# The S5 table stage of a two-block kernel: its transfers issued from GpSimd's queue instead of SP's

## The chip, the cores and the metric

One Trainium2 chip; the kernel uses one core of it. The metric is the device time of the kernel in microseconds. Times of a profile are counted from the start of the profiled execution's span.

## What is computed

Two blocks, one after the other, on a sequence of 512 tokens of width 1024, in fp32. The first is a conformer-like block; the second has retention, an S5 branch and cross-attention:

```python
# first block
x = layer_norm(a*x + 0.5*(1 + g1)*swiglu(modulate(x, sh1, sc1), ffn1...), ...)
...                                     # recurrent and convolution branches, mixed
x = layer_norm(a*x + 0.5*(1 + g3)*swiglu(modulate(x, sh3, sc3), ffn2...), ...)
# second block
ret = retention(q, k, v, ret_gn_g) * silu(g_ret)
ssm = s5_branch(u, a_re, a_im, log_dt, b_re, b_im, c_re, c_im, d, glu_w, glu_b) * silu(g_s5)
x = x + concatenate([ret, ssm]) @ w_out
...                                     # cross-attention on 256 memory tokens
return rms_norm(x, norm_f_g)
```

The S5 branch is a diagonal complex recurrence, of 64 groups with 64 states each:

```python
dt = exp(log_dt)
abar = exp(a*dt)                        # complex: a = a_re + i*a_im
f = (abar - 1) / a
bb = f * b                              # per group, state and input
x[t] = abar * x[t-1] + bb @ u[t]
y = re(c @ x)
```

## The kernel before

**Weights.** Nearly all the time is matmuls of 128x512 tiles in three passes: a weight tile of 128x1024 is loaded raw (512 KB, four buffers, `wr`), ScalarE rounds it to its high part (`wh`, L147), VectorE forms the rest (`wl`, L133), and TensorE multiplies high by high, high by low and low by high: 24 matmuls for one chunk of 128 output columns. `prep` (L165) does this, two chunks ahead of TensorE. Every transfer of the kernel goes through `load` (L129), which issues it from SP, the sync engine. SP takes its list in order: a transfer that waits (a load for a free buffer, a store for the value) holds up all that stand behind it.

**Feed-forward.** `ffn` (L424) runs in three parts of 8, 8 and 6 column blocks. Of each part first the gate and up chunks (two for each block), then eight down chunks. After each chunk `pump` (L251) takes steps of other work from a background list.

**The S5 tables.** The second block's S5 branch needs tables made from a, dt, b and c alone. `s5_tables` (L1041) returns them as steps, put into that list by `after_first` (L977), so they are made under the second feed-forward (877 to 1236 us):

- `small`: loads a_re, a_im and log_dt (two halves) and works out powers of abar and f in some 92 operations, most of 128x32, on VectorE, with two sines on ScalarE. The scheduler puts it much earlier in the program than where it is written.
- `rows`: turns products of the powers with f by TensorE and stores them to DRAM as Fd (four stores).
- `bb`: loads b, makes the input table, stores it as BBd (four), and loads c.
- eight chunks of b: `b_load` loads two tiles from Fd, each row spread over 16 partitions (256 KB), and two tiles of bt as halves (128 KB each); `b_chunk` makes two tiles by six products and sums of 128x512 on GpSimd; `store` stores them to Bd.
- eight chunks of c: `c_chunk` makes two tiles from memsets (L1190) and twelve 64x256 operations on GpSimd; `store` stores them to Cd.

Cd and BBd come back in `s5_kernels` (L1221), for the S5 kernels: its first six reloads of Cd and four of BBd are issued from SP ahead of the last part's down chunks (`before_last`, L1003), and the scheduler moves them into SP's list between weights. The tiles `s` are slots of one pool that all steps share, so a reload waits until the earlier holder of its slot is stored. The order on each engine is the scheduler's, by the program's data flow, not the order of the code.

Of the kernel before, what the change touches and what calls it, by code (L numbers as in the profile page):

```python
# [16 lines left out]
S = 512  # L17
# [1023 lines left out]
def s5_tables(n):  # L1041


    nc, a = n.nc, n.a
    g = nc.gpsimd
    st = {}
    n.Fd = n.DT([2, 8, 32 * 128], "Fd")
    n.Bd = n.DT([8, 2, 128, S], "Bd")
    n.Cd = n.DT([8, 2, 128, S], "Cd")
    n.BBd = n.DT([4, 128, S], "BBd")  # L1050

    def small():
        ar, ai, dt, t, mag, sn, cs, fr, fi = (n.C([128, 32], name="s5") for _ in range(9))
        n.load(ar, a["s5_a_re_2"])
        n.load(ai, a["s5_a_im_2"])
        for p in range(2):
            n.load(dt[p * 64:(p + 1) * 64, :], a["s5_log_dt_2"][p].partition_broadcast(64))
        dt = accurate_exp(n, dt, 32)
        n.tt(mag, ar, dt, ALU.mult)
        mag = accurate_exp(n, mag, 32)  # L1060
        n.tt(fr, ai, dt, ALU.mult)
        reduced(n, fr, t, 32)
        sincos(n, sn, cs, fr)
        P = [n.C([128, 5, 32], name="pw") for _ in range(2)]
        nc.vector.memset(P[0][:, 0, :], 1.0)
        nc.vector.memset(P[1][:, 0, :], 0.0)
        n.tt(P[0][:, 1, :], mag, cs, ALU.mult)
        n.tt(P[1][:, 1, :], mag, sn, ALU.mult)
        t2 = n.C([128, 2, 32], name="pw2")
        for w in (1, 2):  # L1070
            b = [P[j][:, w, :].unsqueeze(1).to_broadcast([128, w, 32]) for j in range(2)]
            cmul(n, P[0][:, 1 + w:1 + 2 * w, :], P[1][:, 1 + w:1 + 2 * w, :], P[0][:, 1:1 + w, :], P[1][:, 1:1 + w, :],
                 b[0], b[1], t2[:, 0:w, :])
        n.s5P = P

        n.q4r, n.q4i = n.C([128, 8, 32], name="q4"), n.C([128, 8, 2, 32], name="q4i")
        Q = n.q4r, n.q4i[:, :, 1, :]
        for j in range(2):
            nc.vector.tensor_copy(out=Q[j][:, 0, :], in_=P[j][:, 4, :])
        s3 = n.A()  # L1080
        t3 = s3[:, 0:128].rearrange("p (k q) -> p k q", k=4)
        for w in (1, 2, 4):
            b = [Q[j][:, w - 1, :].unsqueeze(1).to_broadcast([128, w, 32]) for j in range(2)]
            cmul(n, Q[0][:, w:2 * w, :], Q[1][:, w:2 * w, :], Q[0][:, 0:w, :], Q[1][:, 0:w, :], b[0], b[1], t3[:, 0:w, :])
        n.F(s3)
        n.ts(n.q4i[:, :, 0, :], Q[1], -1.0)
        nP = n.C([128, 4, 32], name="npw")
        n.ts(nP, P[1][:, 0:4, :], -1.0)

        nr = n.C([128, 32], name="nr")  # L1090
        n.ts(nr, P[0][:, 1, :], -1.0, op0=ALU.add)
        ni = P[1][:, 1, :]
        den = mag
        n.tt(den, ar, ar, ALU.mult)
        n.tt(t, ai, ai, ALU.mult)
        n.tt(den, den, t, ALU.add)
        nc.vector.reciprocal(out=den, in_=den)
        n.tt(fr, nr, ar, ALU.mult)
        n.tt(t, ni, ai, ALU.mult)
        n.tt(fr, fr, t, ALU.add)  # L1100
        n.tt(fr, fr, den, ALU.mult)
        n.tt(fi, ni, ar, ALU.mult)
        n.tt(t, nr, ai, ALU.mult)
        n.tt(fi, fi, t, ALU.subtract)
        n.tt(fi, fi, den, ALU.mult)
        st.update(f=(fr, fi), nP=nP)

    def rows():

        P = n.s5P  # L1110
        fr, fi = (x.unsqueeze(1).to_broadcast([128, 4, 32]) for x in st["f"])
        G = [n.A() for _ in range(3)]
        p, h, t = (x[:, 0:128].rearrange("p (k q) -> p k q", q=32) for x in G)
        cmul(n, p, h, P[0][:, 1:5, :], P[1][:, 1:5, :], fr, fi, t)
        for r, x in enumerate((p, h)):
            ps = n.ST()
            for j in range(4):
                n.mm(ps[0:32, j * 128:(j + 1) * 128], x[:, 3 - j, :], n.ident)
            o = n.A()
            n.act(o[0:32, :], ps[0:32, :], AF.Copy)  # L1120
            for p in range(2):
                n.load(n.Fd[r, p * 4:p * 4 + 4].rearrange("k (q x) -> q k x", q=32),
                       o[0:32, :].rearrange("q (k x) -> q k x", k=4))
            n.F(o)
        n.F(G)

    def b_load(ch):

        E, B = ([n.A() for _ in range(2)] for _ in range(2))
        cols = slice(ch * S, (ch + 1) * S)  # L1130
        for r in range(2):
            n.load(E[r], n.Fd[r][:, cols].unsqueeze(1).to_broadcast([8, 16, S]))
            for p in range(2):
                n.load(B[r][p * 64:(p + 1) * 64],
                       a[("s5_bt_re", "s5_bt_im")[r]][ch, p].unsqueeze(0).to_broadcast([4, 16, S]))
        st["b", ch] = E, B

    def b_chunk(ch):
        E, B = st.pop(("b", ch))
        O, T = n.A(), n.A()  # L1140
        n.tt(O, E[0], B[0], ALU.mult, g)
        n.tt(T, E[1], B[1], ALU.mult, g)
        n.tt(O, O, T, ALU.subtract, g)
        n.tt(T, E[0], B[1], ALU.mult, g)
        n.tt(B[0], E[1], B[0], ALU.mult, g)
        n.tt(T, T, B[0], ALU.add, g)
        n.F(E, B)
        st["out", ch] = n.Bd, (O, T)

    def store(ch):  # L1150
        d, X = st.pop(("out", ch))
        for r in range(2):
            n.load(d[ch % 8, r], X[r])
        n.F(X)

    def bb():

        b = [n.A() for _ in range(2)]
        for r in range(2):
            n.load(b[r], a[("s5_bn_re", "s5_bn_im")[r]])  # L1160
        fr, fi = (x.unsqueeze(2).to_broadcast([128, 32, 16]) for x in st["f"])
        br, bi = (x.rearrange("p (c q) -> p c q", q=16) for x in b)
        o = [n.A() for _ in range(3)]
        orr, oi, t = (x.rearrange("p (c q) -> p c q", q=16) for x in o)
        cmul(n, orr, oi, br, bi, fr, fi, t, g)
        for r, x in enumerate((orr, oi)):
            for h in range(2):
                d = n.A()
                g.memset(d, 0.0)
                dv = d.rearrange("p (c r q) -> p c r q", r=2, q=16)  # L1170
                for p in range(2):
                    nc.vector.tensor_copy(out=dv[p * 64:(p + 1) * 64, :, p, :],
                                          in_=x[p * 64:(p + 1) * 64, h * 16:(h + 1) * 16, :])
                n.load(n.BBd[r * 2 + h], d)
                n.F(d)
        n.F(b, o)
        c = [n.A() for _ in range(2)]
        for r in range(2):
            n.load(c[r], a[("s5_c_re", "s5_c_im")[r]])
        n.ts(c[1], c[1], -1.0)  # L1180
        st["c"] = c

    def c_chunk(ch):

        P, nP = n.s5P, st["nP"]
        q = slice(ch * 4, ch * 4 + 4)
        sh = [64, 4, 4, 16]
        X = [n.A() for _ in range(3)]
        for r in range(2):
            g.memset(X[r], 0.0)  # L1190
        for par in range(2):
            d = slice(par * 64, (par + 1) * 64)
            bc = lambda x: x[d].rearrange("p k q -> p q k").unsqueeze(3).to_broadcast(sh)
            pr, pi, npi = bc(P[0][:, 0:4, q]), bc(P[1][:, 0:4, q]), bc(nP[:, :, q])
            cr, nci = (x[d, ch * 64:(ch + 1) * 64].rearrange("p (c x) -> p c x", x=16).unsqueeze(2).to_broadcast(sh)
                       for x in st["c"])
            orr, oi, t = (x.rearrange("p (c r k x) -> p c r k x", c=4, r=2, k=4)[d, :, par] for x in X)
            n.tt(orr, pr, cr, ALU.mult, g)
            n.tt(t, pi, nci, ALU.mult, g)
            n.tt(orr, orr, t, ALU.add, g)  # L1200
            n.tt(oi, pr, nci, ALU.mult, g)
            n.tt(t, npi, cr, ALU.mult, g)
            n.tt(oi, oi, t, ALU.add, g)
        n.F(X[2])
        st["out", 8 + ch] = n.Cd, X[0:2]
        if ch == 7:
            n.F(st.pop("c"))

    work = [(9, lambda ch=ch: b_chunk(ch)) for ch in range(8)] + [(10, lambda ch=ch: c_chunk(ch)) for ch in range(8)]
    steps = [(10, small), (8, rows), (8, bb), (0, lambda: b_load(0))]  # L1210
    for i in range(17):
        if i < 7:
            steps.append((0, lambda i=i: b_load(i + 1)))
        if i < 16:
            steps.append(work[i])
        if i:
            steps.append((0, lambda i=i: store(i - 1)))
    return steps
# [709 lines left out]
```

## Time and profile before

| | |
|---|---|
| three runs | 1840.8, 1843.66, 1845.17 us (median 1843.66) |
| profiled execution, own time | 1847.32 us |
| its span | 1845.5 us |
| granted TensorE clock, mean over the span | 0.988 |
| busy: TensorE, VectorE, ScalarE, GpSimd | 97%, 66%, 37%, 17% of the span |
| HBM read and written | 239 MB and 21 MB, 141 GB/s over the span |
| transfers issued, by engine | all by SP |

The span is the profiled execution from its first to its last instruction; its own time is 1.8 us longer. A share of busy time is an average over stages; for the change the stretch of the second feed-forward, and the start, are read by themselves.

### The profile page before, as it was taken

Reading aid. Unit: us, or ns where it says so; the run is one execution under the profiler, and the core shown is the slowest. Engines: PE = TensorE matmul, PEld = TensorE weight load, DVE = VectorE, ACT = ScalarE, POOL = GpSimd, SP = SyncE. Lnnn points to the kernel's source line nnn. Section 1 sums busy time; section 2 is a strip of 40 time slices with the busy share of each in tenths; the row PEclk is TensorE's granted clock in tenths of the full one; section 3 lists DMA queues with packets and bytes.
Section 4 is the critical chain, followed back from the end, with each engine's and each line's share of the span. In section 5 each row is a group of like instructions: output and inputs, shape, how many; then the busy total and the mean of one; then the engine's idle time right before and its main releaser. Section 6 shows DMA issues by size and latency. Waiting matters only on the chain.

```text
span 1845.5 us, 21756 instructions
## 1 busy us (share of the span) xinstructions
PE 1784.5 (97%) x8242; PEld 1469.6 (80%) x8242; DVE 1219.0 (66%) x1915; ACT 682.9 (37%) x931; POOL 322.7 (17%) x292
## 2 busy tenths in 40 slices
PE   5999999999999999898999999999999999999997
PEld 4888888888877888688887788888888777888886
DVE  7888634378999999768343434357389677356644
ACT  4422323233378522434321222235351223644442
POOL 2000001030000000234145880415000010012102
PEclk9999999999999999899999999999999999999999
DMA  8888432334222223244664444454633225744211
GB/s 319 304 316 319 146 115 97 89 109 146 93 91 69 92 98 113 77 146 136 189 191 132 148 154 152 143 176 102 194 114 102 70 74 171 222 144 131 80 47 57
DMA packets 105352, 261.45 MB, mean 142 GB/s; under 512 B 15008, under 2 KB 32032, under 8 KB 105120
## 3 DMA queue, kind: packets, MB, share of 16 engines
q1 hardware_dynamic: 105248, 260.07, 42.9%
q8 instruction: 64, 1.05, 0.2%
q14 instruction: 40, 0.33, 0.1%
HBM read 239.19 MB, written 20.84 MB: 141 GB/s over the span
## 4 chain that ended last, share of the span: by engine, by line
PE 78%; POOL 7%; DMA 6%; DVE 4%; ACT 2%; issue 2%; SPq 1%; DVEq 0%; POOLq 0%; ACTq 0%
PE ps L152 75%; POOL s L133 6%; PE st L152 3%; DMA s<-in_s_bt_im 2%; DVE s L133 1%; ACT s L147 1%; SPq L130 1%; DMA s<-in_s_bt_re 1%; DVE ar L391 1%; DVE s L136 1%; DMA wr<-in_ffn_w_down 1%; DMA s<-Fd 1%; DMA wr<-in_ffn_w_gate 1%; DVE wl L133 0%; POOL s L143 0%
## 5 line engine op out<-in xcount | busy, mean ns | idle before, releaser
L152 PE MATMUL ps<-s,wh 128*128 128x512 f32 (+1 forms) x4272 | 1324.3, 392 | 11.7 <-ACT wh L147 6.6
L152 PEld LDWEIGHTS ps<-s,wh 128*128 128x128 f32 x4272 | 802.3, 189 | 183.7 <-ACT wh L147 9.9
L152 PE MATMUL ps<-s,wl 128*128 128x512 f32 (+1 forms) x2136 | 832.5, 390 | 3.3 <-DVE wl L133 3.3
L147 ACT ACTIVATE wh<-wr 128x1024 fp32r<-128x1024 f32 (+1 forms) x277 | 289.6, 1047 | 845.5 <-PE ps L152 506.4
L133 DVE TENSOR_TENSOR wl<-wr,wh 128x1024 fp32r<-128x1024 f32 (+1 forms) x277 | 354.2, 1279 | 210.9 <-ACT wh L147 205.6
L152 PEld LDWEIGHTS ps<-s,wl 128*128 128x128 f32 x2136 | 403.4, 189 | 88.8 <-DVE wl L133 5.5
L133 POOL TENSOR_TENSOR s<-s,s 128x512 f32<-128x512 f32 (+2 forms) x152 | 202.5, 1337 | 632.1 <-DVE s L136 326.0
L133 DVE TENSOR_TENSOR s<-s,s 128x512 fp32r<-128x512 f32 (+2 forms) x265 | 205.5, 783 | 55.4 <-ACT s L147 54.3
L147 ACT ACTIVATE s<-s 128x512 fp32r<-128x512 f32 (+3 forms) x246 | 153.2, 637 | 192.5 <-DVE s L133 99.6
L152 PE MATMUL ps<-s,s 128*128 128x512 f32 (+7 forms) x648 | 149.8, 381 | 20.7 <-ACT s L147 18.6
L136 DVE SCALAR_TENSOR_TENSOR s<-s,s,s 128x503 f32<-128x503 f32 (+26 forms) x240 | 164.1, 745 | 0.7
L152 PEld LDWEIGHTS ps<-s,s 128*128 128x128 f32 (+2 forms) x648 | 106.8, 177 | 58.1 <-ACT s L147 21.2
L133 DVE TENSOR_TENSOR s<-s,ps 128x512 f32<-128x512 f32 (+1 forms) x61 | 40.7, 669 | 134.9 <-PE ps L152 134.9
L136 DVE SCALAR_TENSOR_TENSOR s<-ps,c,s 128x512 f32<-128x512 f32 x56 | 41.9, 748 | 82.9 <-PE ps L152 82.7
L391 DVE SCALAR_TENSOR_TENSOR ar<-ar,silc 128x1024 f32<-128x1024 f32 x72 | 89.4, 1252 | 9.7 <-DMA ar<-in_ada_w 9.1
L147 ACT ACTIVATE s<-ps 128x512 f32<-128x512 f32 (+2 forms) x147 | 85.3, 588 | 15.5 <-PE ps L152 15.0
L133 DVE TENSOR_TENSOR s<-ps,s 128x512 f32<-128x512 f32 (+4 forms) x80 | 46.8, 616 | 61.8 <-PE ps L152 41.8
L284 POOL TENSOR_TENSOR gs<-gs,mhalf 128x4 f32<-128x4 f32 x8 | 11.0, 1371 | 259.6 <-DVE gs L141 259.6
L152 PE MATMUL st<-s,s 128*128 128x127 f32 (+2 forms) x368 | 51.5, 297 | 4.4 <-ACT s L147 3.1
L152 PEld LDWEIGHTS st<-s,s 128*128 128x128 f32 x368 | 47.9, 197 | 8.1 <-ACT s L147 3.6
L133 DVE TENSOR_TENSOR s<-s,st 128x512 f32<-128x512 f32 x73 | 46.6, 681 | 11.5 <-PE st L273 11.1
L284 POOL TENSOR_TENSOR ls<-ls,mhalf 128x4 f32<-128x4 f32 x4 | 4.5, 1133 | 259.9 <-DVE ls L136 259.9
(157 smaller groups left out, 884.7 us busy)
## 6 DMA issues: line engine op xcount, KB each, us to landing
wr<-in_w_in SPq DMA_DIRECT2D x80, 512.0 KB
ar<-in_ada_w SPq DMA_DIRECT2D x72, 512.0 KB
wr<-in_ffn_w_gate SPq DMA_DIRECT2D x44, 512.0 KB
wr<-in_ffn_w_up SPq DMA_DIRECT2D x44, 512.0 KB
wr<-in_ffn_w_down SPq DMA_DIRECT2D x32, 512.0 KB
s<-Cd SPq DMA_DIRECT2D x32, 256.0 KB
wr<-in_w_out SPq DMA_DIRECT2D x16, 512.0 KB
wr<-in_ffn_w_down SPq DMA_DIRECT2D x16, 384.0 KB
```

Of the source, the lines that this page charges most:

```text
L130: self.nc.sync.dma_start(out=out, in_=in_)
L133: (eng or self.nc.vector).tensor_tensor(out=out, in0=a, in1=b, op=op)
L136: self.nc.vector.scalar_tensor_tensor(out=out, in0=a, scalar=s, in1=b, op0=op0, op1=op1)
L147: self.nc.scalar.activation(out=out, in_=in_, func=f, scale=scale)
L152: self.nc.tensor.matmul(out, lhsT=lhsT, rhs=rhs, start=start, stop=stop)
L284: self.nc.gpsimd.tensor_tensor(out=out, in0=v, in1=self.mhalf[:, 0:n], op=ALU.pow)
L391: n.nc.vector.scalar_tensor_tensor(out=w, in0=w, scalar=1.0, in1=n.silc, op0=ALU.mult, op1=ALU.mult, accum_out=n.mod[:, j:j + 1])
```

## The change

A helper in `s5_tables` issues a transfer from GpSimd, and every transfer of the stage goes through it: 96 of the 682 that SP had. The reloads of Cd and BBd, and all weights, stay on SP. One line is added, so lines behind L1046 count one higher.

```diff
     g = nc.gpsimd
+    move = lambda out, in_: g.dma_start(out=out, in_=in_)
...
-        n.load(ar, a["s5_a_re_2"])
-        n.load(ai, a["s5_a_im_2"])
+        move(ar, a["s5_a_re_2"])
+        move(ai, a["s5_a_im_2"])
         for p in range(2):
-            n.load(dt[p * 64:(p + 1) * 64, :], a["s5_log_dt_2"][p].partition_broadcast(64))
+            move(dt[p * 64:(p + 1) * 64, :], a["s5_log_dt_2"][p].partition_broadcast(64))
...
         for r in range(2):
-            n.load(E[r], n.Fd[r][:, cols].unsqueeze(1).to_broadcast([8, 16, S]))
+            move(E[r], n.Fd[r][:, cols].unsqueeze(1).to_broadcast([8, 16, S]))
             for p in range(2):
-                n.load(B[r][p * 64:(p + 1) * 64],
+                move(B[r][p * 64:(p + 1) * 64],
                        a[("s5_bt_re", "s5_bt_im")[r]][ch, p].unsqueeze(0).to_broadcast([4, 16, S]))
...
         for r in range(2):
-            n.load(d[ch % 8, r], X[r])
+            move(d[ch % 8, r], X[r])
```

The same replacement is made at the stores of Fd and BBd and at the loads of b and c.

The scheduler then gives other orders. VectorE's list at its start, where `tiny`, `pw`, `m` and `rg` are small constants and vectors and s_6505 is the tile of log_dt:

```order
 L743 MEMSET tiny_2785 128x1
-L1065 MEMSET pw_6586 128x32
-L1066 MEMSET pw_6587 128x32
+L1066 MEMSET pw_6586 128x32
+L1067 MEMSET pw_6587 128x32
+L143 TENSOR_SCALAR s_6505<-s_6505 128x32
 L141 TENSOR_SCALAR m_104<-vecs_84 128x8
 L141 TENSOR_SCALAR rg_2789<-vecs_84 128x8
```

The first operation of `small`, which needs log_dt, now stands ahead of all work on the vectors `vecs`; the others of `small` follow between the sums for the modulation (L391), and ScalarE's two sines move there too. Before, they stood in the first feed-forward.

GpSimd's list in the chunks of b, from the store of one chunk to the first products of another:

```order
+L1046 DMA Bd<-s_7251 128x512
+L1046 DMA Bd<-s_7252 128x512
+L1046 DMA s_7479<-in_s_bt_re 64x1x512 x2
+L1046 DMA s_7478<-Fd 128x1x512
+L1046 DMA s_7595<-in_s_bt_re 64x1x512 x2
+L1046 DMA s_7594<-Fd 128x1x512
+L1046 DMA s_7242<-Fd 128x1x512
 L133 TENSOR_TENSOR s_7372<-s_7242,s_7244 128x512
+L1046 DMA s_7243<-in_s_bt_re 64x1x512 x2
 L133 TENSOR_TENSOR s_7371<-s_7241,s_7243 128x512
 L133 TENSOR_TENSOR s_7371<-s_7371,s_7372 128x512
```

Transfers now stand between the products, some of them loads of later chunks and some, as s_7242 and s_7243, of the product right behind. In this list a transfer also waits for the one eight before it on the same queue, whose semaphore it uses again.

SP's list near the end of the gate and up chunks of the second part, where wr_8074 is the fifteenth of sixteen:

```order
 L130 DMA wr_8005<-in_ffn_w_gate 128x1024
-L130 DMA Cd<-s_8110 128x512
-L130 DMA Cd<-s_8495 128x512
-L130 DMA Cd<-s_8496 128x512
 L130 DMA wr_8038<-in_ffn_w_up 128x1024
 L130 DMA s_9047<-Cd 128x512
 L130 DMA s_9050<-Cd 128x512
 L130 DMA wr_8074<-in_ffn_w_gate 128x1024
-L130 DMA Cd<-s_8233 128x512
-L130 DMA Cd<-s_8234 128x512
-L130 DMA Cd<-s_8616 128x512
+L130 DMA wr_8126<-in_ffn_w_up 128x1024
```

The stores are gone from here; the two reloads of Cd stay where they were, and wait for GpSimd's stores of s_8495 and s_8496, whose slots they take. On GpSimd 55 transfers (12 of Fd, 20 of bt, 16 of Bd, 7 of Cd) stand between the first product of the b chunks and the end of the store of s_8496.

## Rows read from the trace of the kernel before

**Rows 1.** The page, part 1: busy time of each engine, share of the span, instructions

```profile
PE 1784.5 (97%) x8242; PEld 1469.6 (80%) x8242; DVE 1219.0 (66%) x1915; ACT 682.9 (37%) x931; POOL 322.7 (17%) x292
```

**Rows 2.** Five stretches: busy time and instructions of each engine, clock, DMA share, GB/s

```profile
core 0: us, PE busy (x) PEld busy (x) DVE busy (x) ACT busy (x) POOL busy (x), PEclk, DMA share, GB/s
0.00:42.45 42.45, 21.97 (x73) 15.70 (x73) 30.84 (x95) 18.06 (x30) 12.12 (x13) 1.00 0.86 318
913.10:1038.30 125.20, 116.76 (x491) 94.08 (x490) 47.35 (x42) 29.10 (x34) 72.02 (x53) 0.96 0.58 167
1038.30:1101.80 63.50, 63.50 (x282) 52.59 (x281) 24.95 (x22) 15.73 (x20) 58.07 (x74) 1.00 0.36 125
913.10:1087.00 173.90, 165.46 (x706) 134.40 (x705) 67.09 (x59) 41.70 (x50) 116.65 (x107) 0.97 0.51 152
1100.00:1150.00 50.00, 49.01 (x216) 39.95 (x215) 20.09 (x20) 12.59 (x14) 10.16 (x13) 1.00 0.48 170
```

**Rows 3.** The chain of waits, 880 to 1130 us: start us, us, what

```profile
912.51 14.18 DMA s<-in_s_bt_im
...
961.24 12.49 DMA s<-in_s_bt_re
...
991.60 9.84 DMA s<-Fd
...
1010.23 9.79 DMA wr<-in_ffn_w_gate
...
1068.57 2.10 DMA Cd<-s
...
1102.03 3.78 DMA wr<-in_ffn_w_up
```

**Rows 4.** Waits of SP's queue: waited for: us in total, times, longest us

```profile
SPq L130 <- DVE wl L133: 1001.0, 212, 23.5
SPq L130 <- POOL s L133: 142.1, 33, 15.4
```

**Rows 5.** VectorE's timeline, start and near 200 us: start, us, what, [idle before]

```profile
5.86 0.17 DVE L141 TENSOR_SCALAR m<-vecs 128x8 f32<-128x8 f32 x1 [4.78 <-DMA vecs<-in_vecs]
...
197.22 0.18 DVE L143 TENSOR_SCALAR s<-s 128x32 f32<-128x32 f32 x1
197.44 0.18 DVE L143 TENSOR_SCALAR ex<-s 128x32 f32<-128x32 f32 x1
...
207.45 0.19 DVE L133 TENSOR_TENSOR pw<-pw,pw 128x32 f32<-128x32 f32 x1
207.55 0.19 DVE L133 TENSOR_TENSOR ex<-s 128x32 f32<-128x32 f32 x1
...
211.67 0.19 DVE L133 TENSOR_TENSOR s<-s,ex 128x32 f32<-128x32 f32 x1
```

**Rows 6.** SP's timeline, 1015 to 1130 us

```profile
1087.91 1.66 SPq L130 DMA_DIRECT2D s<-Cd  x2
...
1102.03 0.39 SPq L130 DMA_DIRECT2D wr<-in_ffn_w_up  x1
```

**Rows 7.** GpSimd's timeline, 900 to 1180 us

```profile
913.12 1.30 POOL L133 TENSOR_TENSOR s<-s,s 128x512 f32<-128x512 f32 x1 [38.03 <-PE ps L152]
...
1152.65 2.23 POOL L133 TENSOR_TENSOR s<-pw,s 64x256 f32<-64x256 f32 x2 [41.62 <-PE ps L152]
```

**Rows 8.** Issues by tile, Fd and Cd: duration ns min/median/max, first and last start

```profile
L130 SPq DMA_DIRECT2D s<-Fd x16: 577/614/852, 906.4 to 1009.0; - x16
...
L130 SPq DMA_DIRECT2D Cd<-s x16: 319/326/327, 1055.4 to 1174.0; - x16
```

**Rows 9.** The page, part 5: GpSimd's costliest group, busy us, mean ns, idle before

```profile
L133 POOL TENSOR_TENSOR s<-s,s 128x512 f32<-128x512 f32 (+2 forms) x152 | 202.5, 1337 | 632.1 <-DVE s L136 326.0
```

**Rows 10.** TensorE's timeline, at the start and near 1108 us

```profile
22.45 8.57 PE L152 MATMUL ps<-s,s 128*128 128x512 f32 x24 [3.56 <-ACT s L147]
32.43 5.74 PE L152 MATMUL ps<-s,s 128*128 128x512 f32 x24 [1.41 <-ACT s L147]
...
1108.75 0.50 PE L152 MATMUL ps<-s,wl 128*128 128x512 f32 x1 [0.99 <-DVE wl L133]
```

More of the change, by code (lines that the diff above doesn't have):

```diff
@@ L1121, in rows @@
             for p in range(2):
-                n.load(n.Fd[r, p * 4:p * 4 + 4].rearrange("k (q x) -> q k x", q=32),
+                move(n.Fd[r, p * 4:p * 4 + 4].rearrange("k (q x) -> q k x", q=32),
                        o[0:32, :].rearrange("q (k x) -> q k x", k=4))
@@ L1159, in bb @@
         for r in range(2):
-            n.load(b[r], a[("s5_bn_re", "s5_bn_im")[r]])
+            move(b[r], a[("s5_bn_re", "s5_bn_im")[r]])
         fr, fi = (x.unsqueeze(2).to_broadcast([128, 32, 16]) for x in st["f"])
@@ L1173, in bb @@
                                           in_=x[p * 64:(p + 1) * 64, h * 16:(h + 1) * 16, :])
-                n.load(n.BBd[r * 2 + h], d)
+                move(n.BBd[r * 2 + h], d)
                 n.F(d)
@@ L1178, in bb @@
         for r in range(2):
-            n.load(c[r], a[("s5_c_re", "s5_c_im")[r]])
+            move(c[r], a[("s5_c_re", "s5_c_im")[r]])
         n.ts(c[1], c[1], -1.0)
```

## The prediction

> **What bounds the kernel now.** I read the page first: TensorE is busy for 1784.5 of the 1845.5 us span and GpSimd for 322.7 [rows 1]. So a change that touches no matmul can win only where TensorE waits, and can lose wherever it makes TensorE wait. Then I cut the second feed-forward into stretches. From the first product of the Bd tables (913.1 us) to 1038.3 us, TensorE ran 491 matmuls in 125.2 us; in the 63.5 us behind that, 282 at full clock without a pause, 0.2252 us each [rows 2]. At that pitch 491 take 110.6 us: **14.6 us are lost**, partly as idle time, partly at the lower clock that is granted after it (a mean of 0.96 in that stretch). Another 1.0 us is idle between 1100 and 1150 us [rows 2]. The recoverable sum is 15.6 us.
>
> Who lost it? The chain of waits through the same time goes through GpSimd's products and through transfers that take long to land: 14.18 us and 12.49 us for loads of bt, 9.84 us for a load of Fd, and 9.79 us for a weight that stood behind them [rows 3]. The queue's own waits say why weights come late: SP waits mostly for a weight buffer, its usual life (1001.0 us), but for another 142.1 us it waits for GpSimd to finish a product that SP is to store [rows 4], and every weight behind that store waits too.
>
> **What the change takes away.** 96 of SP's transfers go; SP then holds weights and reloads. SP stands no longer in front of a store until the product is there. I take the whole 15.6 us as gone: its places are those where a weight stood behind a table's transfer. The lower end of this gain is nothing, since the same bytes still cross the same DMA engines beside the weights.
>
> **What it adds at the start.** Four loads are GpSimd's first work, and the scheduler moves the short arithmetic on a and dt from 197.22 to 211.86 us, where VectorE had gaps, to the front of VectorE's list, ahead of all that works on the vectors [rows 5]. VectorE had begun there at 5.86 us [rows 5]. Four issues at 1 us from about 0.8 us on, and a landing like the 3.78 us of a weight [rows 3], put dt at 8.6 us: 2.7 us later. The roughly 92 short operations behind it cost 0.1 to 0.2 us each (see their starts in [rows 5]), 9 to 18 us, against 11.6 us that VectorE stood idle in the first 42.45 us [rows 2]. I add 0.8 us for that: **+3.5 us**. The ends are 0 (dt lands before the vectors) and 10 (2.7, and 18 less 11.6 not hidden). At 197 us nothing is won, since TensorE did not wait for it.
>
> **What it adds in the second feed-forward.** This term decides. GpSimd now issues 55 transfers (12 of Fd, 20 of bt, 16 of Bd, 7 of Cd) between its first product and the last Cd store for which SP waits. In SP's order two reloads of Cd, s_9047 and s_9050, come right ahead of wr_8074, the fifteenth of sixteen gate and up chunks of the second part. They go into buffers that GpSimd's tables held and wait for its stores. Before, GpSimd had 57.3 us idle among 173.9 us up to there (116.65 busy) [rows 2], and SP got to the reloads at 1087.91 us [rows 6], with TensorE never stopping for long. Now the list is one after the other on GpSimd:
>
> - the products and memsets, unchanged: 913.1 + 116.65 [rows 2, 7];
> - 55 issues at c each. No row shows a transfer issued by GpSimd. SP took 0.61 us for one of Fd and 0.33 for one of Cd [rows 8]; a GpSimd operation on a whole tile takes 1.34 us [rows 9]. I take **c = 1.0 us**, about the middle of 0.61 and 1.34; the ends are 0.35 and 1.34;
> - landings that nothing covers. Four places: s_7242, s_7243 and s_7477 are loaded right ahead of their products, and the run of issues ahead of s_7242 waits for transfers eight before. At 3.78 us each [rows 3]: 15.1 us. At the low end they are hidden under the issues; at the high end all 57.3 us of idle time stay;
> - the landing of the last store, 2.10 us [rows 3], and 0.4 us for the reload's issue.
>
> That is 913.1 + 116.65 + 55 + 15.1 + 2.5 = 1102.3 us for the issue of wr_8074. From such an issue to steady matmuls it took 6.7 us (1102.03 to 1108.75) [rows 6, 10]: 1109.0 us. TensorE wants it much earlier. Before, it was through with that chunk at about 1107.2 and so began it near 1101.8; with 14.6 us recovered it is there at 1087.2. **The new stall is 21.8 us.** After it the clock is low for a while: after such a pause at the start, 24 matmuls took 8.57 us and the next 24 took 5.74 [rows 10], so +2.8 us.
>
> The Trainium skill, "DMA: Bandwidth & Descriptors", section "Latency and other measured facts", gives about 0.6 us to the first byte from the hardware path and about 1 us from GpSimd's, where it calls the excess the cores' emission. If that 1 us is GpSimd's own time, the sum is the one above; if it is only a delay of the transfer, GpSimd is held for less and the third case below follows. No run here shows it.
>
> Behind that point GpSimd has 9 more Cd stores, about 9 us, and ahead of its last products it stood idle for 41.62 us waiting for TensorE [rows 7]: that covers them, and if it were gone they would hold up the next reloads of Cd in the third part.
>
> **Sum.** 21.8 + 2.8 + 3.5 - 15.6 = +12.5 us. The profiled execution's own time was 1847.32 us, 3.7 above the median of 1843.66; with the sum it would be 1859.8, and against the median **1856 us**. As a formula the change is 55c - 42.5 us: zero at c = 0.77, and 5.5 us for each 0.1 us of c. About 0.2% (3.7 us) is what the measurement can tell from no change.
>
> **Rivals.**
>
> 1. Landings stay as slow as before, and GpSimd waits for them and issues as well. For it: the bt loads are halves of a tile that took 12 to 14 us to land [rows 3], and nothing in the change makes them smaller. Against: they queued behind weights in one queue. All 57.3 us in place of 15.1: +42.2, so 1898 us.
> 2. The other side: an issue costs GpSimd no more than SP. At c = 0.61 the list ends 21.5 us earlier, the new stall is 0.3 us and needs no warming; with +3 at the start, 0.3 + 3 - 15.6 = -12.3, so 1831 us. For it: the same descriptor work, and GpSimd idle a third of the time. Against: every GpSimd operation that shows its cost is slower than its counterpart elsewhere. It decides from c = 0.77 down.
> 3. The change does not do what it says for TensorE: weights land late because the DMA engines are busy, not because of SP's order; GpSimd issues in its idle third, and nothing moves but the start: +3.5 us at most, 1844 to 1847 us. For it: 167 GB/s in the bad stretch against 125 behind it [rows 2]. Against: 318 GB/s at the start [rows 2].
>
> The Trainium skill's page "DMA: Bandwidth & Descriptors", section "Issuing engines are not separate DMA queues", says that an issue from another engine only saves sequencer time, because all run on the same 16 DMA engines. By that rule alone the third case would hold; the 142.1 us of SP standing before stores [rows 4] is sequencer time that the rule itself allows to be saved.
>
> **How the numbers follow.** The forecast, with c between 0.85 and 1.34 (1848 to 1875 us), 0.5; rival 1, 0.2; rival 2, 0.2; rival 3, 0.1. Range: 1829 us, just below rival 2, to 1900, just above rival 1; outside lie c under 0.4 together with hidden landings, and slow landings together with c over 1. The likeliest case's own range is 1848 to 1875. Faster by over 0.2%: 0.2 (rival 2). Within: 0.1. Slower: 0.7 (the forecast and rival 1).
>
> **What would show it.** Right: GpSimd's gaps from 913 us on are about as long as the issues that stand in them; SP waits for GpSimd at the two reloads of Cd for some 15 to 25 us; TensorE shows one long gap near 1087 us, ended by the weight split of wr_8074, and almost none from 913 to 1038. The four issues at 0.8 us come before VectorE's first work on vectors, and steady matmuls begin 2 to 5 us later than 42.45. Wrong: the gap near 1087 is missing (c is small), or TensorE waits for weights between 913 and 1038 as before (rival 3), or GpSimd's idle time ends on loads of Fd and bt rather than on issues (rival 1).

## The result and the profile after

The changed kernel takes **1857.64 us** (median of 4 runs, 1854.63 to 1861.8); the kernel before took 1842.3 us beside it. The ratio is 1.0084, with a 95% interval of 1.0066 to 1.0102: slower by 15 us. The forecast was 1856. The profiled execution is the longest of the four (1861.8 us); it spans 1860.0 us, 14.5 more than that of before.

The page's part 1 and part 3 show what moved: GpSimd is busy for 49 us more, because a transfer that it issues counts as its work, and a second DMA queue exists.

```profile
PE 1782.5 (96%) x8242; PEld 1470.7 (79%) x8242; DVE 1234.6 (66%) x1915; ACT 682.6 (37%) x931; POOL 372.1 (20%) x388
...
q1 hardware_dynamic: 94112, 240.88, 39.2%
q0 software_dynamic: 10368, 19.22, 3.8%
```

**The gain came.** The same stretches as in [rows 2], and one more, of the changed kernel:

```profile
0.00:42.45 42.45, 15.64 (x43) 10.44 (x44) 33.46 (x167) 16.90 (x29) 12.66 (x17) 0.97 0.79 284
...
913.10:1038.30 125.20, 125.20 (x554) 103.66 (x553) 55.66 (x47) 32.24 (x39) 88.51 (x91) 1.00 0.68 180
1038.30:1101.80 63.50, 53.21 (x234) 43.42 (x232) 28.77 (x16) 11.07 (x14) 57.42 (x76) 0.97 0.22 73
...
916.80:1103.10 186.30, 174.71 (x770) 144.03 (x768) 83.65 (x61) 43.31 (x52) 143.90 (x162) 0.99 0.51 142
```

From 913 to 1038 us TensorE does 554 matmuls without a pause, at full clock, where it did 491. In the next stretch it stands still for 10.3 us, where it stood for none. The last row is GpSimd's own list, from its first product to the Cd store that SP waits for: 162 instructions, the 107 of before and the 55 transfers.

**The stall came too.** Waits of SP's queue, against [rows 4]:

```profile
SPq L130 <- DVE wl L133: 1159.3, 241, 23.5
...
SPq L130 <- DMA Cd<-s: 58.6, 4, 46.0
...
SPq L130 <- POOL s L133: 27.6, 7, 10.6
```

The 142.1 us of standing before products are 27.6 now; in their place SP stands once for 46.0 us before a Cd store has landed. The timelines of SP and TensorE show where, against [rows 6, 10]:

```profile
1057.94 0.33 SPq L130 DMA_DIRECT2D wr<-in_ffn_w_up  x1
1104.45 1.17 SPq L130 DMA_DIRECT2D s<-Cd  x2
1105.72 0.37 SPq L130 DMA_DIRECT2D wr<-in_ffn_w_gate  x1
...
1117.30 0.33 SPq L130 DMA_DIRECT2D s<-BBd  x1
...
1093.26 0.39 PE L152 MATMUL ps<-s,wl 128*128 128x512 f32 x1
1111.77 1.22 PE L152 MATMUL ps<-s,wh 128*128 128x512 f32 x2 [18.12 <-ACT wh L147]
```

After the fourteenth weight of the part SP issues nothing from 1058 to 1104 us, because the two reloads of Cd stand first in its list. wr_8074 goes out at 1105.72, and TensorE, which was ready for it at 1093.65, stands for 18.12 us.

**The start came later**, against [rows 5, 10]; timelines of GpSimd, VectorE and TensorE:

```profile
2.58 1.07 POOL L1046 DMA_DIRECT2D s<-in_s_log_dt  x2
...
9.19 0.18 DVE L143 TENSOR_SCALAR s<-s 128x32 f32<-128x32 f32 x1 [8.09 <-DMA s<-in_s_log_dt]
9.28 0.16 DVE L141 TENSOR_SCALAR m<-vecs 128x8 f32<-128x8 f32 x1
...
38.14 7.37 PE L152 MATMUL ps<-s,s 128*128 128x512 f32 x24 [3.28 <-ACT s L147]
```

Behind its first memsets VectorE goes on at 9.19 instead of 5.86 us, with the operation that needs log_dt. A run of 24 matmuls that began at 32.43 begins at 38.14.

The n-th matmul of one trace can be paired with the n-th of the other, each counted from the start of its span. The difference can then be followed through the kernel:

| at, us of the changed kernel | later than before, us | what happened |
|---|---|---|
| 50 to 700 | 7.2 | the start |
| 870 | 7.9 | |
| 890 to 970 | 3.9 | 4.0 won: the kernel before had waited 0.8 and 1.1 us near 876 us, with a granted clock of 0.50 for 3.4 us behind that |
| 1030 | -10.4 | 14.3 won |
| 1060 | -7.9 | 2.4 lost, most of it in a wait of 2.1 us for a weight's split |
| 1111.77 | 10.3 | 18.3 lost in the long gap |
| 1118 | 13.5 | 3.2 lost at a lower clock, some 13 matmuls |
| 1130 | 12.2 | 1.3 won: the kernel before had a short wait of its own |
| the end | 14.3 | |

The row of the slow matmuls behind the gap, with a granted clock of 0.50:

```profile
1111.77:1118.00 6.23, 6.19 (x14) 4.41 (x15) 3.98 (x4) 1.89 (x3) 5.58 (x8) 0.50 0.23 84
```

### The profile page after: what moved, and what is told of

The parts are those of the page before. It is cut to its first block, busy times and chain, and to the rows that moved or that the text cites. A ratio compares the mean times of both kernels' runs of the same rounds, so it can differ in the third digit from the quotient of the medians.

```text
span 1860.0 us, 21759 instructions
## 1 busy us (share of the span) xinstructions
PE 1782.5 (96%) x8242; PEld 1470.7 (79%) x8242; DVE 1234.6 (66%) x1915; ACT 682.6 (37%) x931; POOL 372.1 (20%) x388
## 4 chain that ended last, share of the span: by engine, by line
PE 80%; POOL 8%; DMA 4%; DVE 3%; issue 2%; ACT 1%; SPq 1%; DVEq 0%; POOLq 0%; ACTq 0%
PE ps L152 76%; POOL s L133 6%; PE st L152 3%; DMA s<-Fd 1%; POOL s L1046 1%; DVE s L133 1%; SPq L130 1%; ACT s L147 1%; DVE s L136 1%; DMA Bd<-s 1%; DVE ar L391 0%; POOL Bd L1046 0%; PE st L273 0%; DMA s<-Cd 0%; DMA s<-in_s_log_dt 0%
## 5 line engine op out<-in xcount | busy, mean ns | idle before, releaser
L152 PE MATMUL ps<-s,wh 128*128 128x512 f32 (+1 forms) x4272 | 1321.0, 391 | 21.8 <-ACT wh L147 18.1
L133 DVE TENSOR_TENSOR wl<-wr,wh 128x1024 fp32r<-128x1024 f32 (+1 forms) x277 | 367.3, 1327 | 195.1 <-ACT wh L147 189.3
L133 DVE TENSOR_TENSOR s<-s,s 128x512 fp32r<-128x512 f32 (+1 forms) x265 | 205.1, 782 | 50.0 <-ACT s L147 48.8
L152 PE MATMUL ps<-s,s 128*128 128x512 f32 (+7 forms) x648 | 150.6, 382 | 27.1 <-ACT s L147 23.8
L391 DVE SCALAR_TENSOR_TENSOR ar<-ar,silc 128x1024 f32<-128x1024 f32 x72 | 87.1, 1221 | 8.2 <-DMA ar<-in_ada_w 7.7
L147 ACT ACTIVATE s<-ps 128x512 f32<-128x512 f32 (+2 forms) x147 | 85.2, 587 | 15.5 <-PE ps L152 14.9
```

What stands on the lines that cost most here:

```text
L133: (eng or self.nc.vector).tensor_tensor(out=out, in0=a, in1=b, op=op)
L147: self.nc.scalar.activation(out=out, in_=in_, func=f, scale=scale)
L152: self.nc.tensor.matmul(out, lhsT=lhsT, rhs=rhs, start=start, stop=stop)
L391: n.nc.vector.scalar_tensor_tensor(out=w, in0=w, scalar=1.0, in1=n.silc, op0=ALU.mult, op1=ALU.mult, accum_out=n.mod[:, j:j + 1])
```

## The experiments

Nine kernels, all against the kernel before on the same chip, which took 1841.84 to 1842.35 us each time, so that times of different runs can be set beside each other. Times are medians; the changed kernel took 1857.64 us. Where an expectation says 6.7 us for the later start, the pairing above gives 7.2.

### The start by itself

```diff
-        move(ar, a["s5_a_re_2"])
-        move(ai, a["s5_a_im_2"])
+        n.load(ar, a["s5_a_re_2"])
+        n.load(ai, a["s5_a_im_2"])
         for p in range(2):
-            move(dt[p * 64:(p + 1) * 64, :], ...)
+            n.load(dt[p * 64:(p + 1) * 64, :], ...)
```

> The four loads of `small` go back to SP, the other 92 transfers stay on GpSimd. In the changed kernel TensorE's matmuls run 6.7 us later than before from 47 us on, and I put all of this down to VectorE's list beginning with an operation on log_dt that waits for GpSimd's transfer (until 9.19 us, where the vectors had been there at 5.86). Theory (the start is lost for good, and what follows keeps its distances): steady matmuls begin as before, everything behind them comes 6 to 7 us earlier, 1851 us. Rival (the later stall takes up what the start gives: GpSimd's list begins at a fixed time, TensorE only waits longer near 1090 us): the gap there grows from 18 to about 25 us, and the time stays within 2 us of 1857.6.

Measured: 1851.79 us, ratio 1.0051 (1.0033 to 1.0068). TensorE's start and its waits under the second feed-forward:

```profile
0.00:42.45 42.45, 21.96 (x74) 15.74 (x75) 31.17 (x95) 18.41 (x30) 12.10 (x13) 1.00 0.86 320
```

```profile
PE ps L152 <- ACT wh L147: 17.7, 1, 17.7
```

The start is that of before (21.97 us busy in [rows 2], 21.96 here), and the gap is as long as in the changed kernel: GpSimd's list came earlier with everything else, its first product at 911.28 us instead of 916.83. The start is a loss by itself, of 5.9 us in the median. The rival falls.

### Which reloads stop SP

```diff
     def load():
         st["bb"] = [n.A() for _ in range(4)]
         for i, d in enumerate(st["bb"]):
             n.load(d, n.BBd[i])
         for ch in range(3):
-            fetch(ch)
+            fetch(ch, n.nc.gpsimd)
-    def fetch(ch):
+    def fetch(ch, eng=n.nc.sync):
         st[ch] = [n.A(), n.A()]
         for r in range(2):
-            n.load(st[ch][r], n.Cd[ch, r])
+            eng.dma_start(out=st[ch][r], in_=n.Cd[ch, r])
```

> The first six reloads of Cd are issued from GpSimd as well, so that none of them stands on SP ahead of wr_8074; the reloads of BBd stay on SP, the first of them ahead of the first down chunk, two chunks later. Theory (whatever SP must wait for behind GpSimd's list stops TensorE): the gap ahead of the fifteenth chunk goes, and a gap of 15 to 22 us comes two chunks later, ahead of the first down chunk, because the first reload of BBd waits for a store that GpSimd issued at 1117.6 us; time 1855 to 1860 us, no gain. Rival (only the two reloads of Cd were the trouble): no gap over 5 us, 1833 to 1838 us.

Measured: 1863.99 us, ratio 1.0103 (1.0078 to 1.0128); its profiled execution took 1855.07. TensorE's waits, and SP's timeline:

```profile
PE ps L152 <- ACT wh L147: 17.5, 1, 17.5
```

```profile
1068.20 0.33 SPq L130 DMA_DIRECT2D wr<-in_ffn_w_up  x1
1115.23 0.33 SPq L130 DMA_DIRECT2D s<-BBd  x1
1115.65 1.36 SPq L130 DMA_DIRECT2D wr<-in_ffn_w_down  x3
```

SP gets two weights further (1068.20) and then stands for 47 us before the first reload of BBd. The gap moved by two chunks and is as long. In the end it waits for a product of GpSimd and not, as expected, for the store behind that product: the reload goes out at 1115.23, the store at 1115.50. No gain, as the theory had it, but the median lies above its 1855 to 1860 us. The other executions took about 1863 to 1865 us, some 9 us more than the one with the profile; the trace of that one cannot show why, and it stays open.

Now the reloads of BBd as well:

```diff
         for i, d in enumerate(st["bb"]):
-            n.load(d, n.BBd[i])
+            n.nc.gpsimd.dma_start(out=d, in_=n.BBd[i])
```

> All ten early reloads, six of Cd and four of BBd, are issued from GpSimd; SP then has only weights there. Theory: the two small gaps and the long one near 1090 us (2.2 + 18.4 us) and the slow matmuls behind it (3.2 us) go: 1857.6 - 23.8 = about 1834 us, which is under the 1842.3 of the kernel before. Rival (weights come late because GpSimd's transfers use the same DMA engines, and SP's wait is only where it shows): TensorE waits for weights elsewhere, 1850 us or more.

Measured: **1835.02 us**, ratio 0.9964 (0.9948 to 0.9981). The stretches:

```profile
913.00:1038.00 125.00, 125.00 (x553) 103.48 (x553) 61.76 (x46) 32.09 (x39) 86.61 (x93) 1.00 0.71 180
1038.00:1130.00 92.00, 92.00 (x408) 76.17 (x407) 46.02 (x35) 24.44 (x31) 83.77 (x111) 1.00 0.47 148
```

TensorE does not stop at all in these 217 us. 22.6 us are back, of the 23.8 that the theory counted, with ten more transfers on GpSimd. So neither GpSimd's load nor the sharing of the DMA engines slows TensorE here: ten reloads in SP's list did.

### Does issuing set the pace of GpSimd's list?

```diff
             move(d[ch % 8, r], X[r])
+            if d is n.Bd:
+                move(n.Bx[ch % 8, r], X[r])
```

> Each of the 16 stores of Bd is issued a second time, to another place in DRAM that nothing reads: 16 more issues on GpSimd at 0.60 us, 9.6 us, all ahead of the Cd stores for which SP waits. Theory (GpSimd's list is one after the other, issues and products and waits, and its end sets when wr_8074 may go): the end comes 9 to 11 us later, time 1866 to 1869 us. Rival (landings set the pace and issues lie in their shadow): under 3 us later, 1857 to 1861 us. If more than 13 us are added, the transfers' landings and the rule that each waits for the one eight before cost more than the issues themselves.

Measured: 1862.05 us, ratio 1.0106 (1.0089 to 1.0123): 4.4 us more. SP's timeline:

```profile
1108.06 1.21 SPq L130 DMA_DIRECT2D s<-Cd  x2
```

GpSimd's list, from its first product to the Cd store that SP waits for (in the changed kernel 186.3 us, 143.90 of them busy):

```profile
915.92:1106.74 190.82, 175.59 (x774) 144.76 (x772) 84.56 (x61) 43.34 (x52) 151.08 (x178) 0.98 0.57 161
```

The reloads go out 3.6 us later than in the changed kernel (1104.45). The 16 issues took 9.0 us, 0.56 each, and the list is 4.5 us longer. Neither expectation holds: GpSimd is busy for 7.2 us more and idle for 2.7 us less, so a part of the added issues lies in waits that were there anyway. Its products and memsets read 1.8 us shorter, which stays open. The time is no firm sign here, since its interval overlaps that of the changed kernel (1.0066 to 1.0102); the shift in the trace is.

### Both repairs, and the two halves of the change

The four loads of `small` on SP, all ten reloads on GpSimd:

> The two runs before in one: the loads of `small` back on SP, and all ten early reloads of Cd and BBd on GpSimd. Theory (start and stall are two separate losses that add up): 1857.6 - 5.9 (small alone) - 22.6 (reloads alone) = 1829 us, 13 us under the kernel before. Rival (the reloads on GpSimd already gave all that this stage can give, and an earlier start only makes TensorE wait for something later): 1833 us or more.

Measured: **1828.53 us**, ratio 0.9934 (0.9921 to 0.9947), 13.3 us under the 1841.84 of the kernel before and 29 under the changed one. The two losses add up. The stretch of the stall of before:

```profile
913.00:1038.00 125.00, 125.00 (x554) 103.52 (x553) 66.04 (x44) 32.20 (x38) 86.48 (x90) 1.00 0.66 170
```

With these two repairs in place, one half of the stage's traffic was taken back to SP: first the stores of Bd and Cd.

```diff
-            move(d[ch % 8, r], X[r])
+            n.load(d[ch % 8, r], X[r])
```

> As the run above, but the 32 stores of Bd and Cd go back to SP; the loads of Fd, bt, b and c stay on GpSimd. This asks what cost TensorE its 15 us in the kernel before. Theory (SP standing ahead of stores, 142.1 us in the kernel before, held up weights): the waits come back, 10 to 15 us of the gain are lost, 1839 to 1844 us. Rival (the slow loads that stood ahead of weights in the ring held them up): little is lost, 1829 to 1833 us.

Then, instead, the loads of Fd and bt (three dots stand for what is left out):

```diff
-            move(E[r], n.Fd...)
+            n.load(E[r], n.Fd...)
-                move(B[r]...)
+                n.load(B[r]...)
```

> The other half: the loads of Fd and bt (b_load) go back to SP, the stores of Bd and Cd stay on GpSimd. Theory (SP standing ahead of stores was the loss): the gain stays, 1829 to 1833 us, and the waits of SP for GpSimd stay under 40 us. Rival (the loads in front of weights were the loss): TensorE waits for weights between 913 and 1038 us as in the kernel before, 10 to 15 us, 1839 to 1844 us. If both halves lose about half, each was a part of it.

Measured: 1841.19 us with the stores on SP (0.9998, 0.9989 to 1.0007), 1847.93 us with the loads on SP (1.0042, 1.0026 to 1.0058). The same stretch, first with the stores and then with the loads on SP:

```profile
913.00:1038.00 125.00, 115.35 (x489) 93.86 (x488) 65.49 (x42) 27.43 (x32) 91.79 (x90) 0.96 0.62 171
```

```profile
913.00:1038.00 125.00, 111.72 (x461) 89.76 (x460) 43.77 (x37) 25.76 (x30) 73.83 (x60) 0.93 0.57 160
```

and SP's waits for GpSimd in the two, from 880 to 1140 us:

```profile
SPq L130 <- POOL s L133: 150.0, 27, 24.1
```

```profile
SPq L130 <- POOL s L133: 57.2, 8, 15.1
```

Stores on SP lose 12.7 us of the run before them, loads on SP 19.4. The first run agrees with the theory, the second refutes it: the loads alone are worse, though SP waits less for GpSimd. Neither theory said that either half costs nearly all of the gain or more. A load waits for a buffer that a product of GpSimd frees, a store for a product; either one in SP's list is enough to hold weights back. But the rival of these two runs has its part as well. The chain of waits of the run with the loads on SP goes through weights that were issued right behind loads of Fd and bt and took long to land:

```profile
950.83 14.17 DMA wr<-in_ffn_w_up
...
1012.19 10.57 DMA wr<-in_ffn_w_gate
```

A third took 7.99 us; in the changed kernel the median of such weights is 4.3 to 4.6 us. With the stores on SP the chain of the same time has one weight, of 6.21 us. How much of the 19.4 us is SP's standing and how much is slow landing, no run separates.

### What made GpSimd wait for landings

```diff
-    a[("s5_bt_re", "s5_bt_im")[r]][ch, p].unsqueeze(0).to_broadcast([4, 16, S])
+    a[("s5_bn_re", "s5_bn_im")[r]][p * 64:(p + 1) * 64]
```

> The changed kernel with one thing other: each half load of bt reads 64 whole rows of another input instead of 16 rows four times over, so the result is not the reference's; bytes, issues and the order of all engines stay. It asks what made GpSimd wait 38.7 us for landings where the sum had 15.1. Theory (the spread pattern makes a bt load slow, and the loads of Fd behind it on the same queue with it): GpSimd's waits between its first product and the last needed Cd store fall to 20 us or less, the gap ahead of wr_8074 by 15 us or more, time 1838 to 1843 us. Rival (landings are slow because the weights fill the same DMA engines): waits stay within 5 us of 38.7 and the time within 4 us of 1857.6.

and the same with Fd:

```diff
-            move(E[r], n.Fd[r][:, cols].unsqueeze(1).to_broadcast([8, 16, S]))
+            move(E[r], n.Fd.rearrange("r k (h x) -> (r k h) x", h=8))
```

> As the run above, and each load of Fd reads both halves of Fd once, 128 rows of 2 KB, instead of 8 rows sixteen times over: the same 256 KB, waiting for the same stores; the result is again another. Theory (it is the pattern of bt that is slow, Fd is only behind it): little more than in the run above, within 4 us of it. Rival (Fd's own pattern is slow too): GpSimd's waits fall by another 5 to 10 us, and the time with them. If neither run moves, the landings are set by what shares the engines and not by the patterns.

Measured: 1854.65 us with bt plain (1.0075, 1.0053 to 1.0096), 1841.24 with Fd plain as well (0.9995, 0.9983 to 1.0008). GpSimd's waits for Fd, and Fd's median us from issue to landing (last number), in the changed kernel and in the two runs:

```profile
POOL s L133 <- DMA s<-Fd: 20.6, 4, 8.1
...
s<-Fd POOLq DMA_DIRECT2D x16, 256.0 KB, 6.9
```

```profile
POOL s L133 <- DMA s<-Fd: 17.1, 4, 7.7
...
s<-Fd POOLq DMA_DIRECT2D x16, 256.0 KB, 6.2
```

```profile
POOL s L133 <- DMA s<-Fd: 8.5, 2, 4.5
...
s<-Fd POOLq DMA_DIRECT2D x16, 256.0 KB, 4.4
```

With bt plain, GpSimd's waits for landings, added up over the rows of the view, go from 37.9 us (the 38.7 of the expectation has 0.8 of other waits in it) to 36.9, and the 3 us in time are not clear of the runs' spread: by its numbers the first run gives the rival. The second run refutes the rival, and the theory too: Fd plain as well brings another 13.4 us, and the waits go to 22.4. So Fd's own pattern is slow; Fd plain with bt as it was has not been tried. As many bytes, 256 KB, land in 4.4 us instead of 6.2 when they are read as 128 rows and not as 8 rows sixteen times over. The reloads then go out 15.5 us earlier than in the changed kernel, and of the long gap 0.6 and 0.9 us are left, for a weight's two parts:

```profile
1088.98 0.93 SPq L130 DMA_DIRECT2D s<-Cd  x2
```

```profile
PE ps L152 <- DVE wl L133: 0.9, 1, 0.9
PE ps L152 <- ACT wh L147: 0.6, 1, 0.6
```

(SP's timeline and TensorE's waits from 1060 to 1140 us; a wait of 3.1 us stands at 1029, elsewhere.) The stall hung on these landings.

The Trainium skill, "DMA: Bandwidth & Descriptors", section "Why a DMA increments its semaphore by 16 and not by 1", says that a transfer uses the largest number of engines, up to 16, that divides the slowest dimension on both sides; for some direct copies from GpSimd it names an exception with 16. By that rule a transfer read as 8 rows would use 8 of them and one of 128 rows 16. The packets that the traces keep agree: a load of Fd that stood alone on GpSimd's queue had at most 9 of its 64 packets under way at a time in the changed kernel (issued at 1022.15 us, 2.9 us from the first packet to the last), and up to 15 in the last run (issued at 923.10, 2.0 us). No run separates the number of engines from the reading of the same rows again and again.

## Why the prediction was right, and where it was not

**The frame held.** Slower by one long stall at the two reloads of Cd ahead of wr_8074, and by a later start, against a gain between 913 and 1038 us: all three are in the trace at the places named, and three runs show each by itself (the start, 5.9 us; the reloads, 22.6 us; the gain, which the best run keeps). Predicted +12.5 us; the medians give +15.3, the traces +14.5.

**What was taken away** (15.6 us) came as it was counted: 14.3 in the paired matmuls from 913 to 1038 us (14.6 in the sum) and 1.3 near 1110 (1.0). Another 4.0, ahead of the first product, stood in no term. The part on SP standing ahead of stores was too narrow: the loads on SP hold weights back as well.

**The start** (+3.5 us) was mis-sized: 7.2 in the trace, more than the 2 to 5 that were named as the sign, but inside its ends of 0 and 10 (by its own terms, 2.7 and 18 less 11.6, the upper end is 9.1). The wait for dt was 3.3 us (2.7 in the sum). I counted on 11.6 us of idle VectorE to hide the rest, with 0.8 us over; another 3.9 showed. The new order has the short operations between those that TensorE's first matmuls wait for; what each costs there was not tried.

**The slow matmuls** behind the stall (2.8 us) came as 3.2, at a granted clock of 0.50. But the two runs of 24 matmuls from which the 2.8 was taken stand in a stretch that [rows 2] gives a granted clock of 1.00, so those rows do not show it as the price of a lower clock.

**The stall** (21.8 us) came as 18.3 + 2.4, at 1093.65 us and not near 1087, with SP standing at the reloads for 46.0 us and not the 15 to 25 that were named as the sign. It came by a list whose terms were wrong and cancelled:

| term of the list | predicted, us | measured, us |
|---|---|---|
| first product | 913.1 | 916.8 |
| products and memsets | 116.65 | 110.6 |
| 55 issues | 55 (c = 1.0) | 33.3 (c = 0.61) |
| landings not covered | 15.1 | 37.9 |
| other waits and short gaps | 0 | 4.5 |
| last landing and reload | 2.5 | 2.6 |
| issue of wr_8074 | 1102.3 | 1105.7 |

The issues are told by the tiles' rows, against [rows 8], and the waits by GpSimd's:

```profile
L1046 POOL DMA_DIRECT2D s<-Fd x16: 589/620/649, 911.6 to 1025.6; - x16
...
L1046 POOL DMA_DIRECT2D Cd<-s x16: 539/580/582, 1072.6 to 1187.5; - x16
```

```profile
POOL s L1046 <- DMA Bd<-s: 5.8, 1, 5.8
POOL s L133 <- DMA s<-in_s_bt_re: 3.9, 1, 3.9
POOL s L133 <- DMA Bd<-s: 3.9, 1, 3.9
POOL s L133 <- DMA Cd<-s: 2.3, 1, 2.3
```

(with the 20.6 us for Fd above, and two small ones of 1.4 in all: 37.9; the products are GpSimd's 143.90 busy less 33.3). The step that failed is "I take c = 1.0 us, about the middle of 0.61 and 1.34": GpSimd issues a load of Fd in 0.62 us, as SP did in 0.61, and a Cd store in 0.58, where SP took 0.33. The step "four places, 15.1" failed the other way: a load of Fd makes a product wait for up to 8.1 us, and a load that takes the buffer of a tile just stored stood for 5.8 us until that Bd store had landed, with GpSimd behind it. With c = 0.61 and the rest of the sum unchanged the formula gives 55 x 0.61 - 42.5 = -9 us, the wrong sign. So the number 1856 owes its closeness to two errors of 22 and 23 us against each other, which is luck.

**The rivals.** What came is the forecast's place with a mixture of the first two rivals' terms. Of the 57.3 us of idle time that the first would have kept, 42.4 stayed, 37.9 of them ended by landings: its sign, GpSimd's idle time ending on loads of Fd and bt rather than on issues, is what the trace shows. The second's c of 0.61 came true (an issue took no more than SP's for the loads of Fd, though more for the stores) and its result did not, because of those landings. The third is refuted: TensorE stopped waiting between 913 and 1038 us, and with all ten reloads on GpSimd nowhere from 880 to 1140, though the same bytes were moved. The Trainium skill's rule on issuing engines ("DMA: Bandwidth & Descriptors", "Issuing engines are not separate DMA queues") names as the one thing to be saved the time that a sequencer takes to initiate a transfer, which it calls usually small. What was won here is time that SP stood waiting ahead of a transfer (142.1 us for products before, 27.6 after); the rule does not speak of it, and the prediction read too much into it where it says that the rule allows these 142.1 us to be saved. As to the 1 us to the first byte from GpSimd that the Trainium skill gives ("DMA: Bandwidth & Descriptors", "Latency and other measured facts"): the rows show 0.61 us of GpSimd's time for an issue, so not all of it is the engine's, and what follows is nearer to the second rival's condition.

## What to carry to other kernels

Moving transfers to another queue frees the old one only from those moved; look for what stays behind and depends on them, for a reload left at its old place in the list now waits for a slower producer and holds all that follows. Here that was ten reloads, and moving them too, with four small loads kept where they were, turned 15 us lost into 13 us won. Before a queue is moved, read in the new order what each engine begins with: one operation that waits, put first by the scheduler, delayed the whole kernel by 6 us.

## What the runs showed of the hardware

GpSimd's issue of a transfer took 0.54 to 0.65 us, from 8 KB to 256 KB, save the first of the kernel (0.76) and one load of bt (0.72); I had expected near 1. Sixteen such issues more, 9.0 us, made GpSimd's list 4.5 us longer. The pattern of a load counts: with bt plain in both, 256 KB read as 8 rows sixteen times took 6.2 us to land, as 128 rows 4.4. A weight issued behind such loads in SP's own queue took up to 14.17 us to land.
